# Result stores in the weight-load ring, and another cut of the last weight matrix, in a mixture-of-experts kernel

## The chip, the cores and the metric

The kernel runs on one core of one Trainium2 chip. The time is the device time of one execution in microseconds (us); the median of several runs is compared. One execution was also taken with the hardware profiler.

## The reference

Eight experts each have their own 256 rows of input, and two weight matrices with biases. All tensors are fp32 in HBM.

```
n_experts, capacity, hidden, expert_hidden = 8, 256, 512, 2048
h = np.matmul(x, w1) + b1[:, np.newaxis, :]
h = np.maximum(h, 0)
out = np.matmul(h, w2) + b2[:, np.newaxis, :]
```

Each expert's w1 and w2 are 4 MB in HBM, its x and its result 512 KB.

## The kernel before

The weights are converted to fp16 on the way in: GpSimd issues every weight load as a casting DMA, so they form one queue in the order of issue, which this document calls the ring. A w1 or w2 is 2 MB in SBUF: per partition one row of 16 KB (w2: 16 rows j of 512 columns, next to each other). The x of experts 0 and 1 are loaded in fp32 by SyncE and ScalarE and cast by VectorE; the others come through the ring as well.

An expert's work has two parts. `first_product(e)` (lines 105 to 125) computes hT = relu(w1ᵀ xᵀ + b1) in 16 column groups j; in its middle it transposes x of the next expert on TensorE (`transposes`, line 97). `second_product(e)` (line 139) opens its accumulators with the b2 row (line 151) and adds 32 matmuls of 512 columns over the j rows of w2 (line 163); 256 rows of output make two groups tb of 128. `store` (line 127) copies group 0 from PSUM with VectorE (line 130) and group 1 with ScalarE (line 131) into one result tile, and SyncE issues the store of 512 KB to HBM (line 137).

The main loop (line 223) runs steps s = 0 to 10: first product of expert s, then second product of expert s - 3 (LAG = 3). A list (line 207) sets the order of the ring: x, w1 of expert s, then w2 of expert s - 3, and `issue_until` puts entries into the program two steps ahead. Three buffers each for w1 and w2 set when a load may be issued: GpSimd waits at line 71 for the first product that frees a w1 buffer, at line 82 for the second product that frees a w2 buffer. The order is kept as written (`keep_in_program_order`); instructions of one engine run in order, and a waiting one holds up those behind it. The result tiles have two buffers.

The last two experts' w2 are cut. Expert 6's comes in two halves of 8 rows. Expert 7's comes in pieces with buffers of their own: rows 0 to 4, 4 to 8, 8 to 12 and 12 to 14 in full width, then rows 14 to 16 in two halves of 256 columns. The second product of expert 7 has an accumulator for each half of the columns, so every row costs four matmuls of 256 columns. The left half is copied and stored when its last piece is in, then the right half; each is stored in two transfers of 128 KB, VectorE's group by SyncE (line 134), ScalarE's group by ScalarE itself (line 135).

Of the kernel before, what the change touches and what calls it, by code (L numbers as in the profile page):

```python
# [11 lines left out]
def kernel(  # L12
# [9 lines left out]
    nc = tc.nc  # L22
    fp32 = mybir.dt.float32
    fp16 = mybir.dt.float16
    E, T, H = x.shape
    M = w1.shape[2]
    P = 128
    nTB = T // P
    nKC = H // P
    nJ = M // P  # L30
    HH = H // 2
    LAG = 3
    nXF32 = 2

    def ordered(ins):
        return tc.keep_in_program_order(ins)

    singles = ctx.enter_context(tc.tile_pool(name="singles", bufs=1))
    w1_pool = ctx.enter_context(tc.tile_pool(name="w1", bufs=3))
    w2_pool = ctx.enter_context(tc.tile_pool(name="w2", bufs=3))  # L40
    w2t_pool = ctx.enter_context(tc.tile_pool(name="w2t", bufs=1))
    x_pool = ctx.enter_context(tc.tile_pool(name="xp", bufs=4))
    xT_pool = ctx.enter_context(tc.tile_pool(name="xTp", bufs=2))
    hT_pool = ctx.enter_context(tc.tile_pool(name="hT", bufs=LAG + 2))
    out_pool = ctx.enter_context(tc.tile_pool(name="outp", bufs=2))
    psum_x = ctx.enter_context(tc.tile_pool(name="psum_x", bufs=1, space=bass.MemoryType.PSUM))
    psum_h = ctx.enter_context(tc.tile_pool(name="psum_h", bufs=3, space=bass.MemoryType.PSUM))
    psum_o = ctx.enter_context(tc.tile_pool(name="psum_o", bufs=2, space=bass.MemoryType.PSUM))
# [10 lines left out]
    w1_sb = [None] * E  # L59
    w2_sb = [None] * E  # L60
    hT = [None] * E

    def load_x(e):
        x16[e] = x_pool.tile([P, nTB, H], fp16, tag="x16", name="x16")
        ordered(nc.gpsimd.dma_start(  # L65
            out=x16[e], in_=x[e].rearrange("(p tb) h -> p tb h", tb=nTB)
        ))
# [7 lines left out]
    def load_w2(e):  # L75
        src = w2[e].rearrange("(p j) h -> p j h", j=nJ)
        w2_sb[e] = []
        if e < E - 1:
            t = w2_pool.tile([P, nJ, H], fp16, tag="w2", name="w2sb")
            step = nJ if e < E - 2 else nJ // 2  # L80
            for lo in range(0, nJ, step):
                ordered(nc.gpsimd.dma_start(out=t[:, lo : lo + step, :], in_=src[:, lo : lo + step, :]))  # L82
                w2_sb[e].append((lo, lo + step, 0, H, t[:, lo : lo + step, :]))
            return
        for lo, hi, c0, c1 in (
            (0, 4, 0, H), (4, 8, 0, H), (8, 12, 0, H), (12, 14, 0, H),
            (14, 16, 0, HH), (14, 16, HH, H),
        ):
            t = w2t_pool.tile([P, hi - lo, c1 - c0], fp16, tag=f"w2_{lo}_{c0}", name=f"w2_{lo}_{c0}")
            ordered(nc.gpsimd.dma_start(out=t, in_=src[:, lo:hi, c0:c1]))  # L90
            w2_sb[e].append((lo, hi, c0, c1, t))

    def transposes(e):
        pt = psum_x.tile([P, nKC, T], fp16, tag="psx", name="psx")
        for kc in range(nKC):
            for tb in range(nTB):
                ordered(nc.tensor.transpose(  # L97
                    out=pt[:, kc, tb * P : (tb + 1) * P],
                    in_=x16[e][:, tb, :].rearrange("p (q kc) -> p q kc", kc=nKC)[:, :, kc],
                    identity=ident16,  # L100
                ))
        xT[e] = xT_pool.tile([P, nKC, T], fp16, tag="xT", name="xT")
        nc.vector.tensor_copy(out=xT[e], in_=pt)  # L103

    def first_product(e):
        hT[e] = hT_pool.tile([P, nJ, T], fp16, tag="hT", name="hT")
        for j in range(nJ):
            ph = psum_h.tile([P, T], fp32, tag="ph", name="ph")
            for kc in range(nKC):
                ordered(nc.tensor.matmul(  # L110
                    out=ph,
                    lhsT=w1_sb[e][:, kc, :].rearrange("p (q j) -> p q j", j=nJ)[:, :, j],
                    rhs=xT[e][:, kc, :],
                    start=(kc == 0),
                    stop=(kc == nKC - 1),
                ))
            nc.scalar.activation(  # L117
                out=hT[e][:, j, :],
                in_=ph,
                func=mybir.ActivationFunctionType.Relu,  # L120
                bias=b1T[:, j, e : e + 1],
                scale=1.0,
            )
            if j == nJ // 2 and e + 1 < E:
                transposes(e + 1)

    def store(e, po, c0, c1, split):
        w = c1 - c0
        out_sb = out_pool.tile([P, nTB, w], fp32, tag=f"out{w}", name=f"out{w}")
        nc.vector.tensor_copy(out=out_sb[:, 0, :], in_=po[0])  # L130
        nc.scalar.copy(out=out_sb[:, 1, :], in_=po[1])  # L131
        dst = out[e].rearrange("(p tb) h -> p tb h", tb=nTB)[:, :, c0:c1]
        if split:
            nc.sync.dma_start(out=dst[:, 0, :], in_=out_sb[:, 0, :])
            nc.scalar.dma_start(out=dst[:, 1, :], in_=out_sb[:, 1, :])  # L135
        else:
            nc.sync.dma_start(out=dst, in_=out_sb)

    def second_product(e):
        if e < E - 1:  # L140
            blocks = [(0, H, psum_o, "po")]
        else:
            blocks = [(0, HH, psum_o, "po"), (HH, H, psum_h, "ph")]
        acc = {}
        for c0, c1, pool, tag in blocks:
            for tb in range(nTB):
                t = pool.tile(
                    [P, c1 - c0], fp32, tag=tag if tag == "ph" else f"{tag}{tb}", name=f"acc{tb}"
                )
                acc[c0, tb] = t  # L150
                ordered(nc.tensor.matmul(  # L151
                    out=t,
                    lhsT=ones1,
                    rhs=b2_sb[0:1, e * H + c0 : e * H + c1],
                    start=True,
                    stop=False,
                ))
        for lo, hi, p0, p1, t in w2_sb[e]:
            mine = [b for b in blocks if p0 <= b[0] and b[1] <= p1]
            for tb in range(nTB):  # L160
                for j in range(lo, hi):
                    for c0, c1, _, _ in mine:
                        ordered(nc.tensor.matmul(  # L163
                            out=acc[c0, tb],
                            lhsT=hT[e][:, j, tb * P : (tb + 1) * P],
                            rhs=t[:, j - lo, c0 - p0 : c1 - p0],
                            start=False,
                            stop=(j == nJ - 1),
                        ))
            if hi == nJ:  # L170
                for c0, c1, _, _ in mine:
                    store(e, [acc[c0, tb] for tb in range(nTB)], c0, c1, e == E - 1)

    x32 = singles.tile([P, nXF32, nTB, H], fp32)
    for e in range(nXF32):
# [4 lines left out]
        out=b2_sb,  # L180
        in_=b2.rearrange("e h -> (e h)").rearrange("(o f) -> o f", o=1),
# [10 lines left out]
    for j in range(nJ):  # L192
        for s in range(2):
            ordered(nc.tensor.matmul(  # L194
                out=pb[s * 64 : (s + 1) * 64, j, :, :],
# [5 lines left out]
    for s in range(2):  # L201
        nc.vector.tensor_copy(  # L202
            out=b1T[s * 64 : (s + 1) * 64, :, :], in_=pb[s * 64 : (s + 1) * 64, :, :, s]
        )
    transposes(0)

    loads = []
    for s in range(1, E + LAG):
        if s < E:
            if s >= nXF32:  # L210
                loads.append((load_x, s))
            loads.append((load_w1, s))
        if s >= LAG:
            loads.append((load_w2, s - LAG))
    n = 0

    def issue_until(done):
        nonlocal n
        while n < len(loads) and not done():
            loads[n][0](loads[n][1])  # L220
            n += 1

    for s in range(E + LAG):
        issue_until(lambda: (
            (min(s + 2, E - 1) < E and w1_sb[min(s + 2, E - 1)] is not None)
            and (s + 2 < LAG or w2_sb[min(s + 2 - LAG, E - 1)] is not None)
        ))
        if s < E:
            first_product(s)
        if s >= LAG:  # L230
            second_product(s - LAG)


# [28 lines left out]
```

## Time and profile before

| | us |
|---|---|
| median of 5 runs (lowest to highest) | 186.06 (185.71 to 186.30) |
| the profiled execution | 186.3 |
| its span, first to last instruction | 184.4 |
| TensorE matmuls busy | 138.1 (75%) |
| ScalarE busy | 62.7 (34%) |
| GpSimd busy | 16.9 (9%) |
| VectorE busy | 13.4 (7%) |
| weight-load issue to landing (w1, w2, median) | 33.6, 47.5 |
| store issue to landing on SyncE's queue, 512 KB (median) | 8.4 |
| store issue to landing of the last 128 KB transfers (median) | 2.1 |

How to read it: the profile names engines PE (TensorE matmul), PEld (its weight load), DVE (VectorE), ACT (ScalarE), POOL (GpSimd) and SP (SyncE); a q behind an engine's name is its sequencer, which issues DMAs. L163 is line 163 of the kernel. A line of the timeline has start and duration in us, engine, line, operation, out<-in, shape and count; in brackets stands the idle time before it and what ended that. A digit in the row of slices is the busy share of a fortieth of the span in tenths. A row of a DMA queue has its packets, megabytes written, and the time its packets took as a share of 16 engines' span.

### The profile page before, as it was taken

How to read it: one execution, taken by the hardware profiler on the slowest of the kernel's cores; microseconds unless marked ns; L12 is line 12 of the kernel's file. 1: busy time of each engine (PE TensorE's matmuls, PEld its weight loads, DVE VectorE, ACT ScalarE, POOL GpSimd, SP SyncE). 2: the span in 40 equal slices, each digit the busy share in tenths (PEclk: the TensorE clock that was granted, in tenths of full speed). 3: DMA queues.
4: the chain of work that ended last, by engine and by line, in shares of the span. 5: the costliest groups of instructions: out<-in, count | busy, mean ns of one | idle time of the engine just before them, and what ended most of it. 6: DMA issues, size and time to landing. Idle time of an engine off the chain costs nothing.

```text
span 184.4 us, 2209 instructions
## 1 busy us (share of the span) xinstructions
PE 138.1 (75%) x946; PEld 99.2 (54%) x946; DVE 13.4 (7%) x22; ACT 62.7 (34%) x138; POOL 16.9 (9%) x37
## 2 busy tenths in 40 slices
PE   0546999399631999429995499916999996999971
PEld 0534899289521847328464364805648742434760
DVE  0320011001000110001000101001010010101001
ACT  0022689458540604505136060721507801010101
POOL 7100020300300012000110000100006100100000
PEclk9999999969995799966999799995899999999999
DMA  5998999999999999899999999999899999999993
GB/s 188 281 220 180 228 228 228 194 204 228 229 228 196 203 228 228 170 282 206 199 224 236 261 203 210 228 270 224 188 228 228 218 262 203 244 239 252 221 207 114
DMA packets 6488, 40.57 MB, mean 220 GB/s; under 512 B 688, under 2 KB 1728, under 8 KB 4432
## 3 DMA queue, kind: packets, MB, share of 16 engines
q0 software_dynamic: 4320, 35.14, 91.3%
q1 hardware_dynamic: 1568, 4.46, 6.5%
q10 hardware_dynamic: 592, 0.85, 1.3%
q8 instruction: 7, 0.11, 0.2%
q14 instruction: 1, 0.01, 0.0%
HBM read 71.39 MB, written 4.19 MB: 410 GB/s over the span
## 4 chain that ended last, share of the span: by engine, by line
DMA 57%; PE 31%; another core or an unknown queue 5%; POOL 3%; issue 1%; ACT 0%; ACTq 0%; POOLq 0%
DMA x<-in_x_dram 25%; DMA w<-in_w_dram 20%; PE ph L110 16%; DMA w1sb<-in_w_dram 12%; PE acc L163 12%; PE psx L97 2%; PE acc L151 1%; POOL w2sb L82 1%; POOL w L90 1%; POOL w1sb L71 1%; ACT out L131 0%; POOL b_sb L179 0%; POOL ident masks.py:199 0%; ACTq L135 0%
## 5 line engine op out<-in xcount | busy, mean ns | idle before, releaser
L110 PE MATMUL ph<-xT,w1sb 128*128 128x256 f16 x512 | 68.8, 301 | 8.7 <-DMA w1sb<-in_w_dram 8.5
L117 ACT ACTIVATE hT<-ph,b1T 128x256 f16<-128x256 f32 x128 | 57.0, 475 | 47.3 <-PE ph L110 47.3
L110 PEld LDWEIGHTS <-w1sb 128*128 128x128 f16 x512 | 61.8, 149 | 15.0 <-DMA w1sb<-in_w_dram 9.6
L163 PE MATMUL acc<-w2sb,hT 128*128 128x512 f16 x224 | 49.7, 379 | 2.2 <-DMA w2sb<-in_w_dram 2.2
L163 PEld LDWEIGHTS <-hT 128*128 128x128 f16 x288 | 27.6, 98 | 32.5 <-issue 7.1
L131 ACT COPY out<-acc 128x512 f32<-128x512 f32 (+1 forms) x9 | 4.9, 542 | 60.2 <-PE acc L163 60.2
L97 PE MATMUL psx<-ident,x 128*128 128x128 f16 x64 | 7.0, 276 | 23.9 <-DMA x<-in_x_dram 23.2
L97 PEld LDWEIGHTS <-x 128*128 128x128 f16 x64 | 5.6, 131 | 24.9 <-DMA x<-in_x_dram 24.1
L103 DVE COPY xT<-psx 128x1024 f16<-128x1024 f16 x8 | 5.5, 692 | 86.0 <-PE psx L97 86.0
L130 DVE COPY out<-acc 128x512 f32<-128x512 f32 (+1 forms) x9 | 5.7, 632 | 72.6 <-PE acc L163 72.6
L71 POOL DMA_DIRECT2D w1sb<-in_w_dram x8 | 4.4, 554 | 69.4 <-PE ph L110 68.6
L82 POOL DMA_DIRECT2D w2sb<-in_w_dram x8 | 4.3, 536 | 57.1 <-PE acc L163 57.1
L194 PE MATMUL pb<-ident,b_rows 16*64 16x16 f32 x64 | 3.7, 265 | 6.5 <-DMA b_rows<-in_b_dram 6.5
L163 PE MATMUL acc<-w,hT 128*128 128x256 f16 x64 | 7.5, 272 | 1.1 <-DMA w<-in_w_dram 1.1
L194 PEld LDWEIGHTS pb<-ident,b_rows 16*64 16x64 f32 x64 | 3.6, 198 | 6.5 <-issue 6.5
L117 ACT ACT_TABLE_LOAD x1 | 1.3, 1283 | 10.9 <-DVE b1T L202 10.9
L151 PE MATMUL acc<-b_sb,ones 1*128 1x512 f16 (+1 forms) x18 | 4.8, 355 | 0.0
L90 POOL DMA_DIRECT2D w<-in_w_dram x6 | 3.6, 613 | 12.9 <-DMA w2sb<-in_w_dram 12.9
L65 POOL DMA_DIRECT2D x<-in_x_dram x6 | 3.3, 546 | 0.6 <-DMA w1sb<-in_w_dram 0.6
L151 PEld LDWEIGHTS <-ones 1*128 1x128 f16 x18 | 1.1, 92 | 2.1 <-issue 2.1
L189 DVE CAST x<-x 128x1024 f16<-128x1024 f32 x2 | 1.4, 705 | 4.3 <-DMA x<-in_x_dram 4.3
L202 DVE COPY b1T<-pb 64x128 f32<-64x128 f32 x2 | 0.6, 288 | 3.6 <-PE pb L194 3.6
(8 smaller groups left out, 2.0 us busy)
## 6 DMA issues: line engine op xcount, KB each, us to landing
w1sb<-in_w_dram POOLq DMA_DIRECT2D x8, 2048.0 KB, 33.6
w2sb<-in_w_dram POOLq DMA_DIRECT2D x6, 2048.0 KB, 47.5
out_dram<-out SPq DMA_DIRECT2D x7, 512.0 KB, 8.4
w2sb<-in_w_dram POOLq DMA_DIRECT2D x2, 1024.0 KB, 24.9
x<-in_x_dram POOLq DMA_DIRECT2D x6, 256.0 KB, 40.2
w<-in_w_dram POOLq DMA_DIRECT2D x3, 512.0 KB, 32.3
x<-in_x_dram ACTq DMA_DIRECT2D x1, 512.0 KB, 5.3
x<-in_x_dram SPq DMA_DIRECT2D x1, 512.0 KB, 4.5
```

Of the source, the lines that this page charges most:

```text
L71: ordered(nc.gpsimd.dma_start(out=w1_sb[e], in_=w1[e].rearrange("(p kc) m -> p kc m", kc=nKC)))
L82: ordered(nc.gpsimd.dma_start(out=t[:, lo : lo + step, :], in_=src[:, lo : lo + step, :]))
L90: ordered(nc.gpsimd.dma_start(out=t, in_=src[:, lo:hi, c0:c1]))
L97: ordered(nc.tensor.transpose(out=pt[:, kc, tb * P : (tb + 1) * P], in_=x16[e][:, tb, :].rearrange("p (q kc) -> p q kc", kc=nKC)[:, :, kc] ...
L103: nc.vector.tensor_copy(out=xT[e], in_=pt)
L110: ordered(nc.tensor.matmul(out=ph, lhsT=w1_sb[e][:, kc, :].rearrange("p (q j) -> p q j", j=nJ)[:, :, j], rhs=xT[e][:, kc, :], start=(kc == 0),
L117: nc.scalar.activation(out=hT[e][:, j, :], in_=ph, func=mybir.ActivationFunctionType.Relu, bias=b1T[:, j, e : e + 1], scale=1.0,)
L130: nc.vector.tensor_copy(out=out_sb[:, 0, :], in_=po[0])
L131: nc.scalar.copy(out=out_sb[:, 1, :], in_=po[1])
L151: ordered(nc.tensor.matmul(out=t, lhsT=ones1, rhs=b2_sb[0:1, e * H + c0 : e * H + c1], start=True, stop=False,))
L163: ordered(nc.tensor.matmul(out=acc[c0, tb], lhsT=hT[e][:, j, tb * P : (tb + 1) * P], rhs=t[:, j - lo, c0 - p0 : c1 - p0], start=False, sto ...
L194: ordered(nc.tensor.matmul(out=pb[s * 64 : (s + 1) * 64, j, :, :], lhsT=b1_rows.rearrange("r (q j) -> r q j", j=nJ)[:, :, j], rhs=ident[0 ...
```

## The change

The stores of experts 0 to 4 leave SyncE's queue: `store` notes them in `pending`, and GpSimd issues them in the ring (`flush`). The ring is now a list with the step at which an entry may enter the program. Behind w2 of experts 3, 4, 5 and 6 come the stores of experts 0, 1, 2 and 3; the store of expert 4 comes behind the first piece of expert 7's w2. Experts 5 and 6 are stored by SyncE as before. Result tiles get three buffers.

Expert 7's w2 comes in seven pieces: rows 0 to 4, 4 to 8, 8 to 11, 11 to 13 and 13 to 14 in full width, then rows 14 to 16 with 320 and with 192 columns. Its accumulators and results have 320 and 192 columns. The 320-column result is stored by one SyncE transfer behind both copies; the 192-column result still goes in two, by SyncE and ScalarE.

```diff
-    HH = H // 2
+    HL = 320
     LAG = 3
+    RING = 4
-    out_pool = ctx.enter_context(tc.tile_pool(name="outp", bufs=2))
+    out_pool = ctx.enter_context(tc.tile_pool(name="outp", bufs=3))
+    pending = {}
...
-        for lo, hi, c0, c1 in (
-            (0, 4, 0, H), (4, 8, 0, H), (8, 12, 0, H), (12, 14, 0, H),
-            (14, 16, 0, HH), (14, 16, HH, H),
-        ):
...
+    def flush(e):
+        dst, src = pending.pop(e)
+        ordered(nc.gpsimd.dma_start(out=dst, in_=src))
...
-        if split:
+        if split and c1 == H:
             nc.sync.dma_start(out=dst[:, 0, :], in_=out_sb[:, 0, :])
             nc.scalar.dma_start(out=dst[:, 1, :], in_=out_sb[:, 1, :])
+        elif e <= RING:
+            pending[e] = (dst, out_sb)
         else:
             nc.sync.dma_start(out=dst, in_=out_sb)
...
-            blocks = [(0, HH, psum_o, "po"), (HH, H, psum_h, "ph")]
+            blocks = [(0, HL, psum_o, "po"), (HL, H, psum_h, "ph")]
...
+    ring = []
+    for s in range(1, E + LAG - 1):
+        if s < E:
+            if s >= nXF32:
+                ring.append((s - 2, load_x, (s,)))
+            ring.append((s - 2, load_w1, (s,)))
+        if s >= LAG:
+            ring.append((s - 2, load_w2, (s - LAG,)))
+        if s >= 2 * LAG:
+            ring.append((s - 2, flush, (s - 2 * LAG,)))
+    e = E - LAG - 1
+    for piece in (
+        (0, 4, 0, H), (4, 8, 0, H), (8, 11, 0, H), (11, 13, 0, H), (13, 14, 0, H),
+        (14, 16, 0, HL), (14, 16, HL, H),
+    ):
+        ring.append((0, load_w2_piece, (E - 1,) + piece))
+        if e <= RING:
+            ring.append((e + LAG + 1, flush, (e,)))
+            e += 1
 
     for s in range(E + LAG):
-        issue_until(lambda: (
...
+        while ring and ring[0][0] <= s:
+            _, put, args = ring.pop(0)
+            put(*args)
```

More of the change, by code (lines that the diff above doesn't have):

```diff
@@ L77, in load_w2, with load_w2_piece @@
         w2_sb[e] = []
[L78 to L84, printed above, removed]
-        for lo, hi, c0, c1 in (
-            (0, 4, 0, H), (4, 8, 0, H), (8, 12, 0, H), (12, 14, 0, H),
-            (14, 16, 0, HH), (14, 16, HH, H),
-        ):
-            t = w2t_pool.tile([P, hi - lo, c1 - c0], fp16, tag=f"w2_{lo}_{c0}", name=f"w2_{lo}_{c0}")
-            ordered(nc.gpsimd.dma_start(out=t, in_=src[:, lo:hi, c0:c1]))
-            w2_sb[e].append((lo, hi, c0, c1, t))
+        t = w2_pool.tile([P, nJ, H], fp16, tag="w2", name="w2sb")
+        step = nJ if e < E - 2 else nJ // 2
+        for lo in range(0, nJ, step):
+            ordered(nc.gpsimd.dma_start(out=t[:, lo : lo + step, :], in_=src[:, lo : lo + step, :]))
+            w2_sb[e].append((lo, lo + step, 0, H, t[:, lo : lo + step, :]))
+    def load_w2_piece(e, lo, hi, c0, c1):
+        t = w2t_pool.tile([P, hi - lo, c1 - c0], fp16, tag=f"w2_{lo}_{c0}", name=f"w2_{lo}_{c0}")
+        src = w2[e].rearrange("(p j) h -> p j h", j=nJ)
+        ordered(nc.gpsimd.dma_start(out=t, in_=src[:, lo:hi, c0:c1]))
+        if w2_sb[e] is None:
+            w2_sb[e] = []
+        w2_sb[e].append((lo, hi, c0, c1, t))
     def transposes(e):
@@ L125, in first_product @@
                 transposes(e + 1)
+    def flush(e):
+        dst, src = pending.pop(e)
+        ordered(nc.gpsimd.dma_start(out=dst, in_=src))
     def store(e, po, c0, c1, split):
         w = c1 - c0
-        out_sb = out_pool.tile([P, nTB, w], fp32, tag=f"out{w}", name=f"out{w}")
+        pool = out_pool if w == H else singles
+        out_sb = pool.tile([P, nTB, w], fp32, tag=f"out{c0}_{w}", name=f"out{w}")
         nc.vector.tensor_copy(out=out_sb[:, 0, :], in_=po[0])
@@ L205 @@
     transposes(0)
-    loads = []
-    for s in range(1, E + LAG):
+    ring = []
+    for s in range(1, E + LAG - 1):
         if s < E:
             if s >= nXF32:
-                loads.append((load_x, s))
-            loads.append((load_w1, s))
+                ring.append((s - 2, load_x, (s,)))
+            ring.append((s - 2, load_w1, (s,)))
         if s >= LAG:
[L214 to L221, printed above, removed]
+            ring.append((s - 2, load_w2, (s - LAG,)))
[10 more added lines that the diff above has]
+            e += 1
     for s in range(E + LAG):
-        issue_until(lambda: (
-            (min(s + 2, E - 1) < E and w1_sb[min(s + 2, E - 1)] is not None)
-            and (s + 2 < LAG or w2_sb[min(s + 2 - LAG, E - 1)] is not None)
-        ))
+        while ring and ring[0][0] <= s:
+            _, put, args = ring.pop(0)
+            put(*args)
         if s < E:
@@ L231 @@
             second_product(s - LAG)
+    assert not ring and not pending
 _INS = ['x', 'w1', 'w2', 'b1', 'b2']
```

## The prediction

> **What bounds the kernel now.** I read the page first: busy shares, the slices, the queues.
>
> ```profile
> PE 138.1 (75%) x946; PEld 99.2 (54%) x946; DVE 13.4 (7%) x22; ACT 62.7 (34%) x138; POOL 16.9 (9%) x37
> DMA  5998999999999999899999999999899999999993
> q0 software_dynamic: 4320, 35.14, 91.3%
> q1 hardware_dynamic: 1568, 4.46, 6.5%
> ```
>
> The 16 DMA engines are full from the second slice to the last but one. q0 is GpSimd's ring with all weight loads, q1 is SyncE's queue with the stores. So the time is the engines' work up to the last weight, plus what follows it. TensorE at 75% waits for data; its timeline shows where:
>
> ```profile
> 59.00 1.04 PE L97 MATMUL psx<-ident,x 128*128 128x128 f16 x8 [6.75 <-DMA x<-in_x_dram]
> 82.00 1.04 PE L97 MATMUL psx<-ident,x 128*128 128x128 f16 x8 [6.24 <-DMA x<-in_x_dram]
> 103.94 1.04 PE L97 MATMUL psx<-ident,x 128*128 128x128 f16 x8 [4.75 <-DMA x<-in_x_dram]
> 125.86 1.04 PE L97 MATMUL psx<-ident,x 128*128 128x128 f16 x8 [5.45 <-DMA x<-in_x_dram]
> ```
>
> These are the arrivals of x of experts 4 to 7, one round (a w1, a w2, an x) apart: 23.00, 21.94, 21.92 us, each with one store. Without a store: TensorE gets w1 of experts 2 and 3 at 37.07 and 48.09 (11.02 us for x and w1), and x of expert 4 at 59.00 (10.91 for w2 and x). With x at 1.3 us (below) a bare round is 20.6, so **a store on SyncE's queue costs the ring 1.3 us**: it isn't hidden, the engines do one thing after the other.
>
> The timeline of the end:
>
> ```profile
> 178.55 1.94 PE L163 MATMUL acc<-w,hT 128*128 128x256 f16 x16 [0.47 <-DMA w<-in_w_dram]
> 179.84 0.89 DVE L130 COPY out<-acc 128x256 f32<-128x256 f32 x2 [9.35 <-PE acc L163]
> 180.05 0.37 ACT L131 COPY out<-acc 128x256 f32<-128x256 f32 x1 [7.95 <-PE acc L163]
> 180.29 0.81 SPq L134 DMA_DIRECT2D out_dram<-out  x2
> 180.46 0.37 ACTq L135 DMA_DIRECT2D out_dram<-out  x1
> 180.86 0.37 ACT L131 COPY out<-acc 128x256 f32<-128x256 f32 x1 [0.44 <-PE acc L163]
> 181.27 0.35 ACTq L135 DMA_DIRECT2D out_dram<-out  x1
> ```
>
> Rows 12 and 13 of the last w2 release TensorE at 178.55; 16 matmuls follow without a pause, so both column halves had landed when wanted. The DMA view of 181.1 to 183 us, after an empty 179.6 to 181.1:
>
> ```profile
> q1 hardware_dynamic: 288, 0.26, 42.2%
> q10 hardware_dynamic: 288, 0.26, 41.8%
> ```
>
> Together 84% of 1.9 us: 1.6 us in which all engines pass 512 KB of results without a gap. They begin 0.83 us after the first issue (180.29). So what sets the end is the first issue, not ScalarE's last one.
>
> **The change, part by part.**
>
> *Five stores into the ring.* Bytes and engines stay. Price of 4 KB rows in the ring, from a view in which the ring carries only x (4 KB read per row) beside a store: 100 to 102 us, q0 95 records, 48.5%: 0.485 × 2 × 16 / 95 = 163 ns; eight rows per engine are 1.3 us, as on q1 (94 records, 47.5%: 162 ns). Difference per store 0, bounds ±0.1, five stores ±0.5. All seven stores still run before the last weight, so what the first loads gain (w2 of expert 5 no longer has stores 2 to 4 ahead of it) is given back by then.
>
> Issues: five leave SyncE (0.33 us each) and come to GpSimd (0.53 each, from the w2 rows), an engine 9% busy. What each flush holds up behind it: flush 0 is behind w2 of expert 3, which already waits for the second product of expert 0 (72.12); the copies end 0.4 us later, x of expert 7 waits as long, its transfer is due 50 us later. The same for flush 1 to 3. Flush 4 waits for the second product of expert 4 (ends 153.8) and holds the later w2 pieces; the ring then still has w2 of experts 5 (lands 156.2) and 6, two stores and a piece, 17 us of work. Cost 0; without that cover, the wait itself.
>
> A further wait: GpSimd had up to eight ring transfers open. The 28th issue (145.68) was released when the 20th, w2 of expert 4, landed, the 29th (156.48) by the 21st, the 15th (48.33) by the 7th. With six more issues this matters only if the last piece, now the 35th, met its 27th late: that is flush 3, due at about 166, against 178 when the piece is wanted. 12 us of cover. Result buffers: three; expert 6 copies into the one flush 3 reads, which lands about 1.5 us behind w2 of expert 6, while its copy is wanted 2.2 us behind it. Cost 0 to 0.6 on a VectorE copy that no one waits for.
>
> *Pieces.* The packet records give 324 ns for 4096-byte rows, 172 for 2048, 60 for 512 (69 records at 48.9% in 179.0 to 179.5: 57 with completions), about 15 ns of each overlapping the next. So 42 for 512, 159 for 2048, 307 for 4096: some 6 + 0.0735 per byte. New rows: 3072 bytes 232, 1024 bytes 82, 640 bytes 53, 384 bytes 34. Per engine, before: 3 × 8 × 307 + 8 × 159 + 16 × 42 = 9.3 us to the first half's landing, +0.67 to the second's. After: 2 × 8 × 307 + 8 × 232 + 8 × 159 + 8 × 82 + 16 × 53 = 9.55, +0.54. **The 320 columns land 0.25 later, the last 192 about 0.1 later.** The bytes bound it: between 512 and 16384 bytes a byte costs 0.074 to 0.082 ns, ±0.1 in all. 384 bytes lie below every load row of the trace: from 34 (by bytes) to 60 a packet, 0 to +0.4 for the last 192 columns only.
>
> The Trainium skill speaks against such rows: DMA: Bandwidth & Descriptors, Specifications, wants at least 512 B per transfer for line rate, below which the engine reads, modifies and writes. No 384-byte load stands in the trace; doubled by that rule, 16 × 34 would be 0.5 us more for that piece, an estimate.
>
> *The end.* By the completion records the column halves landed at 179.19 and 179.84. New: 179.44 and 179.94. TensorE is not late: rows 11 to 13 take 12 matmuls of 256 columns on average, 1.3 us, and land 1.5 and 0.85 us ahead of the 320 columns; done by 179.3. Then four matmuls of 320 columns (0.109 for 256, 0.216 for 512: 0.136) and 0.3 us of pipeline: 179.47 + 3 × 0.136 + 0.30 = 180.18. ScalarE copies 320 columns in 0.43 (0.37 for 256, 0.59 for 512), from 180.21 to 180.64, and only then may SyncE issue, as the one store waits for both copies: 180.68 against 180.29, **+0.39**. Before, VectorE's half left alone and opened the chain; that is what the merged store gives up. The other block: 179.97, four matmuls of 192 columns, done 180.5, copy to 180.95, ScalarE issue 180.98, earlier than 181.27 because the issue between its copies is gone: −0.3, but its packets queue behind the 320 columns' in the same 1.6 us.
>
> The 320-column store has 256 rows, not 128. Before's one SyncE transfer of 256 rows, x at the start, was issued at 0.74 and its first packet came at 1.85: 1.10 us against 0.83. Between 0 and +0.27, I take **+0.13**: it was a cold start.
>
> Sum: 0.39 + 0.13 = **+0.5 us**; pieces are inside the 0.39. Span 184.4 + 0.5 = 184.9, the profiled time 186.3 (1.9 around the span) becomes 186.8; that execution stood 0.24 over the median of 186.06, so I forecast 186.55.
>
> **The rivals.**
>
> *ScalarE's chain sets the end.* The page's chain ends ScalarE copy, issue, copy. If the four results did not fill the engines, the last issue would count: 180.98 against 181.27, −0.3, time 185.75. Against it: 84% in the two rows above.
>
> *The first store's stretch goes (the other side).* The round with the first store is 23.00, the next two 21.94 and 21.92: 1.06 us more. Windows of equal phase agree: 69 to 78 us moved 194 GB/s, 92 to 101 us 223. If SyncE's first store into a full ring causes it and a ring store doesn't, −1.06 + 0.5 = −0.55, time 185.5. It decides if all engines keep 223 GB/s through the first store. Against: stores 2 to 7 on the same queue show no such thing, and SyncE still has experts 5 and 6.
>
> *The ring stops at each store.* A store writes to HBM, and a result took 2.1 us from issue to landing, some 0.5 after its last packet. If the ring held later packets until such a write is confirmed, 5 × 0.5 = +2.5 on the +0.5: 189.0. For it: no store in the ring is in this trace. Against: on q1 the engines went on past completions, at 1.3 us a store. The Trainium skill (DMA: Bandwidth & Descriptors, Queues, rings and completion order) says that the completion write lands after the engine's earlier writes, across queues, not that later data waits; so by it, nothing.
>
> **How the numbers follow.** About 0.2% (0.37 us) is what a measurement of this kernel can tell from no change. Forecast 0.54: own range 186.1 to 187.1 (start of 256 rows, ring price ±0.5, piece rows ±0.1), of which 0.42 slower, 0.12 same. ScalarE's chain 0.17: 0.13 same, 0.04 faster. Stretch gone 0.21: 0.19 faster, 0.02 same. Ring stops 0.08, slower. Faster 0.23, same 0.27, slower 0.50. The range, 185.4 to 187.1, takes in the stretch at its price and the forecast's own bounds; it leaves out the ring stopping and what lies beyond the bounds of the others, under 2 in 10.
>
> **What would show it.** Right: SyncE's 320-column issue is the first of the three last stores, 0.4 us later after its piece than now; then about 1.6 us of full engines; rounds between x arrivals keep 21.9 where a store lies in them, 20.6 where none does (the rounds ending with x of experts 5 and 6 lose theirs); DMA slices stay at 9. Wrong: a last weight landing off 179.9 by over half a microsecond, TensorE pausing between last pieces, a gap on q0 behind a flush, or a GpSimd wait past 170 us.

## The result and the profile after

The changed kernel takes **186.48 us** in the median (186.16 to 187.17 over 39 runs), the kernel before 186.05 (65 runs beside it): a ratio of **1.0024**, 95% interval 1.0018 to 1.003, so +0.43 us. Forecast were 186.55 and +0.5. The profiled execution took 186.78 with a span of 185.0, 0.30 above the median; that of before 186.3 with 184.4.

The page of the changed kernel, busy time, slices and queues:

```profile
PE 140.8 (76%) x946; PEld 100.2 (54%) x946; DVE 13.3 (7%) x22; ACT 62.9 (34%) x138; POOL 20.1 (11%) x43
DMA  5999999999999999999999999999999989999963
q0 software_dynamic: 5184, 37.76, 94.4%
q1 hardware_dynamic: 976, 2.00, 3.1%
q10 hardware_dynamic: 448, 0.69, 1.0%
```

The engines are as full as before. q0 rose from 35.14 to 37.76 MB, which is five stores of 0.52 MB that left q1; 3.4% of the span left q1 and 3.1% came to q0.

The timeline of TensorE, x of experts 4 to 7 arriving:

```profile
59.11 1.04 PE L98 MATMUL psx<-ident,x 128*128 128x128 f16 x8 [6.75 <-DMA x<-in_x_dram]
79.79 0.64 PE L98 MATMUL psx<-ident,x 128*128 128x128 f16 x8 [3.29 <-DMA x<-in_x_dram]
100.44 0.64 PE L98 MATMUL psx<-ident,x 128*128 128x128 f16 x8 [3.80 <-DMA x<-in_x_dram]
122.79 1.04 PE L98 MATMUL psx<-ident,x 128*128 128x128 f16 x8 [5.51 <-DMA x<-in_x_dram]
```

The rounds are 20.68, 20.65 and 22.35 us, where before had 23.00, 21.94 and 21.92. Without a store a round is 20.65, as forecast (20.6). The round that now holds the first store is 22.35, that is 1.70 above a bare one; before's first one was 2.35 above.

The timeline of the end, first of TensorE alone:

```profile
169.02 1.91 PE L171 MATMUL acc<-w,hT 128*128 128x320 f16 x16 [0.76 <-DMA w<-in_w_dram]
173.10 6.98 PE L171 MATMUL acc<-w,hT 128*128 128x320 f16 x48 [2.18 <-DMA w<-in_w_dram]
```

Then of the other engines:

```profile
179.52 0.79 DVE L136 COPY out<-acc 128x320 f32<-128x320 f32 x2 [12.74 <-PE acc L171]
179.79 0.65 ACT L137 COPY out<-acc 128x320 f32<-128x320 f32 x2 [11.41 <-PE acc L171]
180.24 0.62 SPq L145 DMA_DIRECT2D out_dram<-out  x1
180.47 0.38 ACTq L141 DMA_DIRECT2D out_dram<-out  x1
180.91 0.59 SPq L140 DMA_DIRECT2D out_dram<-out  x1
```

From rows 4 to 8 of the last w2 onwards, TensorE runs 48 matmuls without a pause: it no longer waits for each piece but is behind them. The first issue of the last results (180.24, line 145) is the first of three, as forecast, and stands where before's stood (180.29). The issue itself takes 0.62 us; before's two took 0.81 together.

The DMA view of 181.5 to 183.3 us, after an empty 179.2 to 181.5:

```profile
q1 hardware_dynamic: 416, 0.43, 69.6%
q10 hardware_dynamic: 144, 0.10, 17.1%
```

Together 86.7% of 1.8: 1.56 us of full engines, the forecast 1.6. But they begin 1.26 us after the first issue, not 0.83.

The end, from the completion records and the closing rows of the two profiled executions (us from the span's start; the last two columns are differences):

| | last weight landed | last matmul done | first issue of last results | last result landed | span | issue to landing | landing to span's end |
|---|---|---|---|---|---|---|---|
| before | 179.84 | 180.48 | 180.29 | 183.32 | 184.35 | 3.03 | 1.03 |
| changed | 179.10 | 180.08 | 180.24 | 183.65 | 184.97 | 3.41 | 1.32 |

The last column is called the closing below: what the engines still do, mostly waiting for each other, when all results have landed. So +0.62 of span is made of −0.05 at the first issue, +0.38 from there to the landing, and +0.29 of closing. The forecast had +0.39, +0.13 and nothing: the sum came out right from other terms. The experiments look for each.

One more term lies outside the span. The device time is longer than the span by 1.94 us in the profiled execution of before and by 1.81 in that of the changed kernel; over all recorded runs the mean is 1.94 to 1.95 and 1.78. So some 0.16 of what the span grew by is not in the time. The forecast took 1.9 as fixed; why it shrank, no run shows.

### The profile page after: what moved, and what is told of

It reads as the page before. It is cut to its first block, busy times and chain, and to the rows that moved or that the text cites. A ratio compares the mean times of both kernels' runs of the same rounds, so it can differ in the third digit from the quotient of the medians.

```text
span 185.0 us, 2204 instructions
## 1 busy us (share of the span) xinstructions
PE 140.8 (76%) x946; PEld 100.2 (54%) x946; DVE 13.3 (7%) x22; ACT 62.9 (34%) x138; POOL 20.1 (11%) x43
## 3 DMA queue, kind: packets, MB, share of 16 engines
q0 software_dynamic: 5184, 37.76, 94.4%
## 4 chain that ended last, share of the span: by engine, by line
DMA 71%; PE 23%; POOL 2%; issue 1%; ACT 1%; ACTq 0%; POOLq 0%
DMA x<-in_x_dram 24%; DMA w2sb<-in_w_dram 24%; DMA w1sb<-in_w_dram 12%; PE acc L171 11%; DMA w<-in_w_dram 11%; PE ph L111 11%; PE psx L98 1%; ACT out L137 1%; PE acc L159 1%; POOL w1sb L73 1%; POOL out_dram L130 0%; POOL b_sb L187 0%; POOL ident masks.py:199 0%; POOL ident masks.py:197 0%; ACTq L137 0%
## 5 line engine op out<-in xcount | busy, mean ns | idle before, releaser
L111 PE MATMUL ph<-xT,w1sb 128*128 128x256 f16 x512 | 70.9, 307 | 8.4 <-DMA w1sb<-in_w_dram 8.4
L111 PEld LDWEIGHTS <-w1sb 128*128 128x128 f16 x512 | 62.9, 150 | 15.6 <-DMA w1sb<-in_w_dram 9.4
L171 PEld LDWEIGHTS <-hT 128*128 128x128 f16 x288 | 28.1, 100 | 34.1 <-issue 7.4
L137 ACT COPY out<-acc 128x512 f32<-128x512 f32 (+2 forms) x9 | 4.8, 541 | 62.0 <-PE acc L171 62.0
L98 PE MATMUL psx<-ident,x 128*128 128x128 f16 x64 | 6.2, 254 | 20.0 <-DMA x<-in_x_dram 19.4
L98 PEld LDWEIGHTS <-x 128*128 128x128 f16 x64 | 5.0, 125 | 21.1 <-DMA x<-in_x_dram 20.3
L136 DVE COPY out<-acc 128x512 f32<-128x512 f32 (+2 forms) x9 | 5.6, 633 | 76.7 <-PE acc L171 76.7
L171 PE MATMUL acc<-w,hT 128*128 128x320 f16 (+1 forms) x64 | 8.9, 307 | 2.9 <-DMA w<-in_w_dram 2.9
L159 PE MATMUL acc<-b_sb,ones 1*128 1x512 f16 (+2 forms) x18 | 4.8, 355 | 0.0
L130 POOL DMA_DIRECT2D out_dram<-out x5 | 2.7, 538 | 19.4 <-ACT out L137 13.1
```

The costliest lines, as they stand in the source:

```text
L98: ordered(nc.tensor.transpose(out=pt[:, kc, tb * P : (tb + 1) * P], in_=x16[e][:, tb, :].rearrange("p (q kc) -> p q kc", kc=nKC)[:, :, kc] ...
L111: ordered(nc.tensor.matmul(out=ph, lhsT=w1_sb[e][:, kc, :].rearrange("p (q j) -> p q j", j=nJ)[:, :, j], rhs=xT[e][:, kc, :], start=(kc == 0),
L159: ordered(nc.tensor.matmul(out=t, lhsT=ones1, rhs=b2_sb[0:1, e * H + c0 : e * H + c1], start=True, stop=False,))
L171: ordered(nc.tensor.matmul(out=acc[c0, tb], lhsT=hT[e][:, j, tb * P : (tb + 1) * P], rhs=t[:, j - lo, c0 - p0 : c1 - p0], start=False, sto ...
```

## The experiments

They ran in three groups, each beside runs of the kernel before (medians 186.12, 186.1 and 186.03). Ratios are to these.

**Splitting the 320-column store again** (on the changed kernel):

```diff
-        if split and c1 == H:
+        if split:
```

> The changed kernel, with its 320-column result stored in two transfers again (VectorE's group by SyncE, ScalarE's by ScalarE). Theory A (the merged store is dear: it leaves 0.2 us later than VectorE's half could, and its first packet comes 1.26 us after the issue, not 0.83): first packets at about 180.9 in place of 181.5, end 0.5 us earlier, median about 186.0. Theory B (the end belongs to TensorE, which in the profiled execution was late and at half clock, and a store is a store): the last issue moves little, 186.4 to 186.5. ScalarE's issue between its copies returns (+0.37 on that engine); if that decides the end, 186.3.

Measured: 186.4 us, ratio 1.0018 [1.0009, 1.0026]; span 184.7. SyncE's issues of the last results in its timeline:

```profile
179.97 0.81 SPq L140 DMA_DIRECT2D out_dram<-out  x2
```

The first issue stands at 179.97 and the last landing at 182.96: 3.0 us, as before. Yet the span ends 1.76 us later. The store's gain, which Theory A expected, comes back in the closing, which the changed kernel had at 1.32 and before at 1.03. So the median is Theory B's number, but not for its reason.

**Merging the left store alone** (on the kernel before):

```diff
-        if split:
+        if split and c1 == H:
```

> The kernel before, with the left 256 columns of the last expert stored in one SyncE transfer behind both copies; nothing else. Theory A: first issue 0.17 us later (after ScalarE's copy, 180.46 for 180.29), first packet 1.26 for 0.83 us behind it: +0.5 to +0.6, 186.6. Theory B: 186.0 to 186.1. If only the lateness of the issue counts: +0.2, 186.25.

Measured: 186.8 us, 1.0036 [1.0024, 1.0048]. From the timeline of its end, VectorE, ScalarE and SyncE:

```profile
180.09 0.91 DVE L130 COPY out<-acc 128x256 f32<-128x256 f32 x2 [9.65 <-PE acc L163]
180.31 0.86 ACT L131 COPY out<-acc 128x256 f32<-128x256 f32 x2 [8.26 <-PE acc L163]
180.71 0.62 SPq L137 DMA_DIRECT2D out_dram<-out  x1
181.20 0.37 ACTq L135 DMA_DIRECT2D out_dram<-out  x1
```

The first issue moves from 180.29 to 180.71, but only 0.17 of this +0.42 is the wait for both copies: from the start of VectorE's copies to the first issue it is 0.62 us here (180.09 to 180.71) and 0.45 in before (179.84 to 180.29). The other 0.25 came with the weights, the last of which landed at 180.12 in this execution, 0.28 later than in before. From the first issue to the last landing it is 3.41 instead of 3.03. Wait and start of the store together are 0.55, as Theory A had it. The median rose by 0.68, more than by the whole change.

**The pieces and 320 columns alone** (on the kernel before, all stores split and on SyncE):

```diff
-    HH = H // 2
+    HH = 320
...
-            (0, 4, 0, H), (4, 8, 0, H), (8, 12, 0, H), (12, 14, 0, H),
+            (0, 4, 0, H), (4, 8, 0, H), (8, 11, 0, H), (11, 13, 0, H), (13, 14, 0, H),
```

> The kernel before, with the seven pieces and 320 + 192 columns, each result in two transfers, all stores on SyncE's queue. As predicted for the pieces alone: last weight 0.1 us later, 320 columns 0.25 later, shorter second block: -0.1 to +0.3, 186.0 to 186.3. If smaller pieces make TensorE pause and lose its clock: TensorE ends 0.5 to 1 us behind the last landing, 186.5 or more. If they help as a shorter last step: 185.8.

Measured: 186.4 us, 1.0015 [1.0007, 1.0024], so +0.28. The profiled execution doesn't show it: last weight at 179.68, last landing at 183.17, span 184.2, all a little earlier than before's. Its span is the shortest of the eleven runs, whose median span is 184.4 against 184.2 for before. So the cause of the +0.28 stays open: the profile shows neither the forecast's +0.25 for the 320 columns nor anything in its place. The pieces do not gain.

**The five ring stores alone** (on the changed kernel, old pieces, old split):

```diff
-    HL = 320
+    HL = H // 2
...
-        if split and c1 == H:
+        if split:
...
-        (0, 4, 0, H), (4, 8, 0, H), (8, 11, 0, H), (11, 13, 0, H), (13, 14, 0, H),
+        (0, 4, 0, H), (4, 8, 0, H), (8, 12, 0, H), (12, 14, 0, H),
```

> The changed kernel with the old pieces (4, 4, 4, 2 rows and two halves of 256 columns) and every last result in two transfers: the five ring stores alone. Prediction on record: a ring store costs what a SyncE store costs, 186.05 with bounds of 0.5. From the changed kernel's trace (last weight 179.10 for 179.84, the first store's stretch 0.4 for 1.06 us): the last weight lands 0.7 to 0.8 us earlier, 185.4 to 185.6 if TensorE keeps up. If TensorE, held up by the store of expert 4 between two pieces, loses its clock: 185.9 to 186.2.

Measured: 186.7 us, 1.0028 [1.0019, 1.0037]; span 184.8. The last weight lands at 179.03, 0.81 earlier than before, and the time is still 0.5 longer. Two things carry it, TensorE and the closing. TensorE's timeline:

```profile
173.08 1.91 PE L171 MATMUL acc<-w,hT 128*128 128x256 f16 x16 [2.18 <-DMA w<-in_w_dram]
176.46 3.65 PE L171 MATMUL acc<-w,hT 128*128 128x256 f16 x32 [1.47 <-DMA w<-in_w_dram]
```

Rows 8 to 12 start it at 176.46, and 32 matmuls run on to 180.1, so the last weight at 179.03 waits for TensorE, not TensorE for it. The last landing is at 182.98, 0.34 earlier than before, and then the closing takes 1.87 instead of 1.03. The time lies above what was expected either way: TensorE was late without losing its clock (see below), and the closing was in no expectation.

The three parts run alone cost some +0.7, +0.3 and +0.5, together 1.5, and the change costs 0.43. They do not add, so none of them is a price of its share in the change.

**TensorE kept at full clock** (18 unread matmuls of 256 columns behind the first piece of the last w2):

```diff
+            if e == E - 1 and lo == 0:
+                warm = psum_h.tile([P, T], fp32, tag="ph", name="warm")
+                for _ in range(18):
+                    ordered(nc.tensor.matmul(
+                        out=warm, lhsT=hT[e][:, 0, 0:P], rhs=hT[e][:, 1, :], start=True, stop=True,
+                    ))
```

> The changed kernel, with 18 matmuls that nobody reads (256 columns, 0.109 us each, 2.0 us) behind the first piece of the last w2, where TensorE otherwise waits 2.18 us for rows 4 to 8. Theory A (that pause costs TensorE its clock: 0.50 granted from 173 to 176.4 us, the 48 matmuls that follow take 6.98 in place of 5.3 us, and TensorE ends a microsecond behind the last weight): with the clock kept the last weight (179.1) is the bound, last matmul at 179.6 in place of 180.1, median 0.3 to 0.5 lower, 186.0 to 186.15. Theory B (the clock fell only in the profiled execution, or the end hangs on the last weight anyway): 186.4 to 186.5.

The windows 172 to 174, 174 to 176 and 176 to 178 us of the changed kernel show why this was tried; the third number from the end, ahead of the DMA share and GB/s, is the granted clock:

```profile
172.00:174.00 2.00, 0.90 (x5) 0.64 (x5) 0.00 (x0) 0.00 (x0) 0.00 (x0) 0.74 1.07 300
174.00:176.00 2.00, 2.00 (x11) 1.35 (x10) 0.00 (x0) 0.00 (x0) 0.00 (x0) 0.50 1.09 231
176.00:178.00 2.00, 2.00 (x19) 1.59 (x18) 0.00 (x0) 0.00 (x0) 0.00 (x0) 0.91 1.12 165
```

In before the same three windows have 1.00. After the pause of 2.18 us TensorE runs 11 matmuls in 2 us instead of some 20. But the pause alone doesn't decide it: the run with the ring stores alone paused as long (2.18 us ahead of 173.08) and kept its clock:

```profile
174.00:176.00 2.00, 0.99 (x10) 0.73 (x8) 0.00 (x0) 0.00 (x0) 0.00 (x0) 1.00 1.04 249
```

And the profiled execution of the changed kernel is no typical one: its mean granted clock, 0.912, is the lowest of all its recorded runs (the others 0.918 to 0.939). With the unread matmuls all three windows are at full clock; the last of them:

```profile
176.00:178.00 2.00, 1.63 (x16) 1.22 (x15) 0.00 (x0) 0.00 (x0) 0.00 (x0) 1.00 1.11 177
```

and TensorE waits for pieces again, as its timeline shows:

```profile
177.63 2.51 PE L171 MATMUL acc<-w,hT 128*128 128x320 f16 x20 [0.37 <-DMA w<-in_w_dram]
```

Measured: 186.5 us, 1.0024 [1.0014, 1.0033]: no different from the changed kernel, as Theory B had it. In this execution the last weight came at 179.59 and the last matmul ended 0.55 later, against 0.98 in the changed kernel; its clock stood at 0.50 earlier, from 154 to 156 us. By the difference of 0.98 and 0.55, an estimate, the half clock costs some 0.4 us in that one profiled execution; it is not what makes the median longer.

**Twelve more GpSimd instructions at the start** (on the kernel before):

```diff
+    spare = singles.tile([P, 1], fp32)
+    for _ in range(12):
+        nc.gpsimd.memset(spare, 0.0)
```

> The kernel before, with 12 memsets of a [128, 1] tile more on GpSimd at the start, where it idles. In the closing of the program GpSimd stands still for 0.33 to 0.42 us in the three profiles with ring stores and in none of the three without (last result landed to the end of the span: 1.32 us after, 1.04 before). Theory A (it comes from a longer GpSimd program): +0.3 to +0.4, 186.4. Theory B (it belongs to the ring stores, or to chance): 186.1.

This asked whether the closing depends on how many instructions GpSimd has run. In the recorded rows of the changed kernel, GpSimd takes its first closing wait at 183.82 and its next row only at 184.26, while SyncE and the rest stand behind it; in before these rows lie 0.07 apart. The late row is the 69th recorded one of GpSimd, and so it is in every kernel with ring stores up to here; before has only 63. With twelve more (75 rows) the 69th is the closing wait itself, and a stop ahead of it would fall into the wait. Measured: no such gap, closing 1.04 as in before, but 186.38 us, 1.0015 [1.0005, 1.0025]. The median is Theory A's number without the gap that Theory A is about. The profiled execution, the slowest of the twelve runs (186.91), has the last weight at 180.30 instead of 179.84, behind a round of 22.58 us between x of experts 6 and 7 instead of 21.92; why, and whether that makes the median's +0.28, was not found. So the row's number tells where GpSimd stands still; what that costs this run can't tell.

**An early first store** (on the kernel before: 128 rows of 512 B of zeros into a part of expert 7's result, which is written again at the end):

```diff
+    zero = singles.tile([P, 128], fp32)
+    nc.vector.memset(zero, 0.0)
+    nc.sync.dma_start(out=out[E - 1].rearrange("(p tb) h -> p tb h", tb=nTB)[:, 0, 0:128], in_=zero)
```

> The kernel before, with one store more at the very start, 128 rows of 512 bytes of zeros into a part of the last expert's output that the real result overwrites at the end. The round with the first result store took 0.9 to 1.06 us more than the later ones in three profiles with SyncE stores, 0.3 to 0.5 in three with ring stores. Theory A (the first write to the output tensor costs all engines something, once): paid at the start where the engines idle, the round falls from 23.0 to 21.9, median 185.1 to 185.5. Theory B (a store that meets a full ring for the first time costs it, whatever was written before): 186.1. Theory C: it is paid before the first w1, 186.1, with the round at 21.9 and the first product later by as much.

Measured: 186.2 us, 1.0003 [0.9994, 1.0012], nothing, so Theory A is out. The round with the first big store is 22.59 us, 0.2 to 0.4 below the other four kernels whose stores all go through SyncE (22.80 to 23.00), and still 0.65 above 21.94. But x of expert 4 came at 59.44 instead of 59.00, so the round ends where it did. A small first write doesn't take the stretch away; whether it moved part of it to the start, as Theory C has it, is open.

**One store fewer in the ring** (expert 4's on SyncE, on the changed kernel):

```diff
-    RING = 4
+    RING = 3
```

> The changed kernel with the store of expert 4 on SyncE's queue, four in the ring: nothing stands between the first and the second piece of the last w2, and that store has run 10 us earlier. Theory A (the store between the pieces makes TensorE pause and lose its clock): rows 4 to 8 come about 1.3 us sooner, the pause is 0.9 in place of 2.2 us, clock 1.00, 0.3 to 0.5 lower than the changed kernel, 186.0 to 186.15. Theory B (where the store stands is indifferent, as all engines' work is the same): 186.45.

Measured: 186.9 us, 1.0042 [1.003, 1.0054], above both theories. Theory A's steps are there: TensorE pauses for 0.64 us at most between the pieces and is at full clock, it is done at 179.85, and the first issue is at 180.01, 0.23 earlier than in the changed kernel. But the closing grew to 1.72. That placed the second part of the closing. With expert 4's store SyncE's and ScalarE's queues carry nine transfers, as in the split version and with the ring alone (closings 1.76 and 1.87); the changed kernel has eight. In the recorded rows these transfers share eight semaphores in turn, and SyncE waits for one after the other at the end, some 0.06 us each. The ninth transfer comes to the semaphore that is waited for first, so all the others are asked after the last landing; with eight, the last landing is the one asked last.

**Three more GpSimd instructions** (on the changed kernel):

```diff
+    spare = singles.tile([P, 1], fp32)
+    for _ in range(3):
+        nc.gpsimd.memset(spare, 0.0)
```

> The changed kernel with three memsets of a [128, 1] tile more on GpSimd at the start. In five profiles with ring stores GpSimd stands still for 0.35 to 0.5 us between its 68th and 69th recorded row, wherever that falls: in the closing of the program there; before has 63 rows, and with twelve memsets more (75 rows) the 69th fell behind GpSimd's long wait for the end and nothing was seen. Theory A (something at the 69th row, such as code that has to be fetched): with three rows more it falls ahead of that wait, the closing shrinks by 0.4 (last result landed to end of span 1.32 to 0.9 us), median 186.05 to 186.1. Theory B (it belongs to ring stores, whatever the row): 186.45.

Measured: **186.04 us**, 0.9997 [0.9988, 1.0006], so 0.44 less than the changed kernel and level with before. The closing is 0.92 instead of 1.32, without a gap in GpSimd's rows: Theory A. (This profiled execution was its fastest, 185.60, with TensorE at full clock from 168 us on; the medians are what counts.)

**Eight transfers with the store split** (the split version, and x of experts 0 and 1 in one SyncE transfer instead of one each):

```diff
-        if split and c1 == H:
+        if split:
...
-    for e in range(nXF32):
-        (nc.sync if e == 0 else nc.scalar).dma_start(...)
+    nc.sync.dma_start(
+        out=x32.rearrange("p e tb h -> p e (tb h)"),
+        in_=x[0:nXF32].rearrange("e (p tb) h -> p e (tb h)", tb=nTB),
+    )
```

> The changed kernel with both last results in two transfers, as in the earlier run, and the x of experts 0 and 1 in one SyncE transfer: eight transfers in all on the queues of SyncE and ScalarE, not nine. With nine, the last store shares the first of eight semaphores that SyncE asks for one after the other at the end (0.06 us each), so seven follow its landing. Theory A (that order counts): 1.75 us from landing to end become 1.35, median 0.4 below the run with nine, 186.0. Theory B (the waits cost nothing together): 186.4. x comes at most 1 us later, ahead of the first w1 all the same.

Measured: 185.68 us, 0.999 [0.9981, 0.9999], below both theories: 0.72 less than the split version by the medians, some 0.5 by the ratios, as the two ran beside different runs of the kernel before (186.12 and 186.03). Issue to landing 3.01, closing 1.33 instead of 1.76. The closing explains 0.43; the rest may be the merged load of x, which wasn't run by itself.

**Expert 4's store behind the last weight** (on the changed kernel, the flush behind all pieces):

```diff
-        if e <= RING:
-            ring.append((e + LAG + 1, flush, (e,)))
-            e += 1
+    ring.append((e + LAG + 1, flush, (e,)))
```

> The changed kernel with the ring store of expert 4 as the last entry of the ring, behind all pieces of the last w2. Before and after the change all engines idle for 1.3 to 2.4 us between the last weight and the first packet of the last results, as long as one store takes. Theory A (that store is hidden there): last weight 177.8 in place of 179.1, TensorE no longer paused for 2.2 us and done at about 178.4 to 178.8, end 1.0 to 1.6 us earlier, median 184.9 to 185.5. Theory B (it meets the last results, the engines are busy as long as before): at most 0.4 earlier, 186.05.

Measured: 185.3 us, 0.9959 [0.9947, 0.9972], 1.18 less than the changed kernel, close to the price of a store in the ring: Theory A. The first issue of the last results:

```profile
178.81 0.61 SPq L145 DMA_DIRECT2D out_dram<-out  x1
```

The last weight lands at 178.10 and the store behind it at 179.40, in the time in which the engines were empty while TensorE, the copies and the issue follow the last weight; the first packet of the last results comes after it, at 180.07.

**All of it** (split store, x in one transfer, three GpSimd instructions, expert 4's store last; the edits are those shown):

> The three together on the changed kernel, with every last result in two transfers: store of expert 4 last in the ring, eight transfers on SyncE's and ScalarE's queues, three memsets more on GpSimd. If the parts add: store hidden -1.3, first packets of the results 0.4 earlier, closing 0.9 to 1.0 us: 184.2 to 184.8. If the hidden store meets the earlier results: 185.0 to 185.4.

Measured: **184.05 us**, 0.9894 [0.9881, 0.9908], 1.1% below before and 1.3% below the changed kernel. The parts measured in medians are −0.08 (split), −0.44 (GpSimd), −0.72 (eight transfers) and −1.18 (store last): −2.42 from 186.48 is 184.06. These four do add, also by the ratios, which give 184.15. The timeline of its end:

```profile
174.34 4.06 PE L171 MATMUL acc<-w,hT 128*128 128x320 f16 x32 [0.95 <-DMA w<-in_w_dram]
...
178.35 0.81 SPq L140 DMA_DIRECT2D out_dram<-out  x2
178.56 0.88 ACTq L141 DMA_DIRECT2D out_dram<-out  x2
```

The last weight lands at 177.81, the first issue follows at 178.35, the last landing at 181.35 (3.0) and the closing takes 0.92. TensorE runs its last 32 matmuls without a pause and ends at 178.40, so it is now as late as the weights.

The closing in all the profiled executions, by GpSimd's recorded rows and the number of transfers on SyncE's and ScalarE's queues:

| kernels | GpSimd rows | GpSimd stands still in the closing | transfers | closing |
|---|---|---|---|---|
| left store merged alone | 63 | no | 13 | 1.09 |
| before; pieces alone; twelve more GpSimd instructions | 63; 64; 75 | no | 14 | 1.03 to 1.04 |
| early first store | 63 | no | 15 | 0.97 |
| three more GpSimd instructions; all of it | 77 | no | 8 | 0.92 |
| changed; full clock; eight transfers; store last | 74 | yes | 8 | 1.32 to 1.34 |
| split again; ring stores alone; one store fewer | 74; 73; 72 | yes | 9 | 1.72 to 1.87 |

With 13, 14 and 15 transfers the last one has the fifth, sixth and seventh of the eight semaphores, so three, two and one are asked after it, and the closing differs by 0.06 from each to the next. With eight, none is asked after it; with nine, seven are.

## Why the prediction was right, and where by luck

- **Price of a store in the ring**: right. A bare round is 20.65; moving one store behind the last weight gave 1.18 to the median, against 1.3 forecast. By the completion records the stores of experts 1, 2 and 4 landed 1.27 to 1.32 us behind the load ahead of them; that of expert 3 took 1.88, beside packets of a SyncE store. The ring doesn't stop at stores: q0 fills 94.4% of the span, and +2.5 us are nowhere.
- **Issues and waits of the flushes**: right in their size. GpSimd's timeline:

```profile
152.31 0.54 POOL L130 DMA_DIRECT2D out_dram<-out  x1 [13.09 <-ACT out L137]
...
154.62 0.53 POOL L89 DMA_DIRECT2D w<-in_w_dram  x1 [0.70 <-DMA out_dram<-out]
...
166.22 0.71 POOL L89 DMA_DIRECT2D w<-in_w_dram  x1 [1.17 <-DMA out_dram<-out]
```

  The flush of expert 4 waits 13.09 us for its ScalarE copy, under the work queued in the ring; the last piece waits for a store's landing and goes out at 166.22, where "about 166" stood as the date of the eighth transfer behind.
- **Pieces**: packet prices right (3072 bytes 247 ns, 1024 bytes 98, 640 bytes 69, 384 bytes 51 as recorded, some 15 of each overlapping; forecast 232, 82, 53, 34). 51 ns for 384 bytes against 60 for 512: the penalty below 512 B, weighed against the change from the Trainium skill (DMA: Bandwidth & Descriptors, Specifications), isn't seen here (384 bytes are what a row writes to SBUF; in HBM it has 768). But the date of the last weight, 179.94, was wrong: 179.10. The step that failed is the one that let only the bytes move it. The stretch of the first store shrank from 1.06 to about 0.4 (22.35 − 21.94), and most of the 0.74 by which the last weight came earlier than before's is there. The runs of the parts agree: with the ring stores alone the last weight lands at 179.03, with the pieces alone at 179.68. So the rival of the other side came true by a bit over half its price; why a store in the ring stretches less is open.
- **"TensorE is not late"**: wrong, from one missing step. In the order of the ring, expert 4's store (landed 170.28) and, from SyncE's queue, that of expert 6 (packets from 171.85 to 174.70) fall among the first pieces, which starves TensorE for 2.18 us ahead of rows 4 to 8; from its release 48 matmuls are left in the 6.0 us to the last weight. In the profiled execution the last matmul ended 0.98 us behind the last weight, before's 0.64. The first of them also ran at a clock of 0.50, but that does not follow from the order alone: with the ring stores alone the same pause left the clock at 1.00, and TensorE still ended 1.08 us behind the last weight. The Trainium skill (TensorE: Matmul & The Clock Gate, Part 1) says that the clock halves after an idle window of about 3.4 us; here it was at half for 3.41 us behind a pause of 2.18, so the length of a pause does not tell by itself.
- **First issue, +0.39**: mis-sized in the sum. The wait for both copies is there: from the start of VectorE's copies to the first issue it is 0.17 more where the store alone is merged on the kernel before, and 0.20 more in the changed kernel (0.72) than in its split version (0.52). Most of the rest of the term was the 0.25 by which the 320 columns were to land later than before's first half (179.44 for 179.19). They landed at 178.58, with TensorE behind them: the first issue came at 180.24 instead of 180.68.
- **Start of a 256-row store, +0.13**: mis-sized, +0.43. 1.26 us to the first packet against 0.83 (180.24 to 181.50; 180.29 to 181.12). From issue to landing the six merged kernels take 3.39 to 3.41, the split ones 2.99 to 3.04, but for the one with twelve more GpSimd instructions (3.33). The upper bound, from x at the start, was 0.27: marking it down for a cold start was wrong, and the bound itself was too low.
- **Closing**: the step that wasn't there. The sum ended with the last landing, and the 1.03 behind it was taken as fixed. It became 1.32, since GpSimd, with eleven more rows, stands still in it; three rows more, whose result nobody reads, take the closing to 0.92 and the change's +0.43 back to −0.01. So the stall is 0.40, and 0.11 less of waits, with eight transfers instead of 14, stands against it.
- **The rivals**: ScalarE's chain is out: the last issue of all, now SyncE's at 180.91, came 0.36 earlier than before's (ScalarE's at 181.27), and the time didn't follow. The stretch shrank in part. The ring doesn't stop.

Of the four signs that the prediction named for being wrong, two came true: the last weight landed 0.84 off its date, and TensorE paused between the last pieces. The forecast held all the same, since errors at the first issue (−0.44), at the store's start (+0.30), in the pass of the results (−0.05), at the closing (+0.29) and outside the span (−0.13) came to −0.03 together. The price of a store in the ring and the covered waits were right by their mechanism; the end came out right by luck.

## What to carry to other kernels

Put into the ring behind the last load whatever does not have to be done before it: the gap between the last weight and the first result packet held a whole store for nothing (−1.18 us of 186). Read a change's cost up to the end of the span, not up to the last landing: waits, code and the number of transfers sit there, and a few tenths decide at this size. Two transfers of 128 rows, each issued as its engine is ready, were better than one of 256 rows that waits for both, but only once their number did not lengthen the closing: −0.08 us in the median with nine transfers, 0.5 to 0.7 less again with eight.

## What the runs showed of the hardware

- **The first large store stretches its round**: by 0.9 to 1.06 us where it goes through SyncE's queue (rounds of 22.80 to 23.00 against 21.94), by 0.6 at most in the ring (21.87 to 22.57 in nine kernels, so not at all in the shortest). With a small store ahead of it the round was 22.59. A later round can be longer too: 22.37 for the second one where the store alone is merged, 22.58 for the third with twelve more GpSimd instructions. What makes it is open.
- **A store of 128 partitions by two rows takes longer to begin**: issue 0.61 to 0.62 us and first packet after 1.26, in all six kernels that have one, against 0.33 and 0.83 with one row of each partition.
- **GpSimd stands still 0.40 to 0.44 us ahead of its 69th recorded row** when that lies in the closing, in all seven kernels where it does. One of the trace's two instruction queues has one 8 KB read at 45 to 49 us in all these kernels, and a second one which falls near the span's end in those that stand still (185.21 in the changed kernel) but at 167.45 and 169.49 with three rows more. (Without a gap in the closing it fell at 182.92 with twelve more on the kernel before, and at 186.08, behind the span, with the pieces alone, which have 64 rows.) The Trainium skill (Runtime: NRT & Kernel Launch, Instruction fetch mechanics) says that engines fetch their code in blocks of 16 KiB while they run, mostly hidden. The reads fit that but for the size, 8 KB on this queue (the other reads 16 KB at a time); that the stall is the wait for the code isn't shown, as the late read is recorded behind it.
- **Small rows**: rows that write 384 bytes cost 51 ns in the ring, in line with the 59 to 69 ns of 512 and 640 bytes.
